# One two-layer diffusion backbone: element-wise work taken off GpSimd, context products moved inside their groups, deeper first loads, the residual loaded by job

## The chip, the core and the metric

The kernel runs on one core of a Trainium2 chip. The metric is the device time of one execution in microseconds (us), from the first to the last instruction and what lies around them; the median of several executions counts. Engines are named as the profile names them: PE is TensorE's matrix products (PEld its weight loads), DVE VectorE, ACT ScalarE, POOL GpSimd, and SP is SyncE, whose queue issues most DMAs.

## What is computed

1024 latent tokens and 256 context tokens of width 1024 pass two layers, all in float32. Layer 0 mixes by four retention heads and four attention heads (two key/value heads) out of one projection; layer 1 by a spatial-gating MLP. Each is followed by a squared-ReLU MLP of width 4096.

```python
def reference(x, c, ctx, c_ctx, mod_w, mod_b, norm1_g, ...):
    for l in range(DEPTH):
        mod_lat = (silu_c @ mod_w[l] + mod_b[l])[:, None, :]      # sh1, sc1, g1, sh2, sc2, g2
        h_lat = modulate(rms_norm(x, norm1_g[l]), sh1, sc1)
        if is_even:
            o_lat, o_ctx = mix_ab(h_lat, h_ctx, ab_w_in[i], ab_w_out[i], ret_decay[i], ...)
        else:
            o_lat = mix_chunk_mlp(h_lat, cm_w_in[i], ...)
        x = x + g1 * o_lat
        x = x + g2 * sq_relu_mlp(modulate(rms_norm(x, norm2_g[l]), sh2, sc2), ff_w1[l], ff_w2[l])

def retention_chunkwise(q, k, v, log_gamma, state0):          # chunks of 128, forward and backward
    scores = jnp.einsum('bnihd,bnjhd->bnhij', qc, kc) * decay
    intra = jnp.einsum('bnhij,bnjhe->bnihe', scores, vc)
    chunk_kv = jnp.einsum('bnjhd,jh,bnjhe->nbhde', kc, k_decay, vc)
    state -> chunk_decay * state + kv_n ;  cross = q @ state_prev * q_decay
```

The first retention state comes from the context tokens; retention and attention queries and keys of the latent tokens are rotated (rotary embedding). Of layer 0 only the latent stream is needed further, so the context runs through the projections alone.

## The kernel before

Every large float32 product is made of three products of rounded pairs (`mm3`, L74: high by high, high by low, low by high). A split into the pair is one ScalarE cast (L80) and one subtraction (L81).

*Start (L106 to L283).* SyncE loads the context, the eight latent tiles `x_t` and sixteen tiles `mw` of the first modulation matrix (two parts of eight; 512 KB each, three buffers, `mod_row`, L235), between them four weight tiles `st` of group 0. TensorE sums the modulation rows (`modrow`), `mod_cols` (L115) turns them into columns; VectorE and ScalarE form squares, and normalise (L266), shift and split the tokens into `hc` (context) and `hl` (latent) (L268 to L280). Of eight row tiles two are split by ScalarE, ScalarE and GpSimd, the others by ScalarE and VectorE.

*Projection groups (L348 to L561).* Six groups: four retention heads (`r_group`) and two key/value groups (`a_group`). `p_group` loads the group's four weight pairs into a ring of twelve tiles, then makes the context's products `pc` (48 instructions) and the latent ones `pl` in four steps `tp` of 48 instructions (two row tiles each), with two accumulators in turn. `lat_evac` empties an accumulator: VectorE makes two rotary products out of it, GpSimd adds them (L485). GpSimd also scales values by their decay (`vc`, L467, of the context; `vk`, L496, of the latent tokens). `tick` advances generators that run beside the group: `heads` of the retention head before, and the transposes `tal`, `tac` of the attention groups.

Between the products of groups 1 to 5 `mod_run` (L156) advances a further generator: 90 steps, ten times eight loads of a 512 KB modulation tile into one of three staging buffers `st`, each with a VectorE multiply-add (`macc`, L139), and a closing step of transposes and sums (`mcol`). The weights use the same three buffers. Two and three steps follow the products of a step `tp` in turn.

*Attention, output product, MLPs.* Scores `s` of attention begin while the last transposes are made. In each layer the MLP's up half writes the hidden tiles to DRAM, seven forms each (`s_d`), out of a ring `ur` of sixteen buffers; the down half (`mlp_down`, L869) reads them back (`sT`, `sB`, L877), multiplies them with seven forms of its weights in jobs (q, p0, p1) and adds each product to the residual `xd` (L882). The residual's eight tiles lie in the space of `ur` and are loaded by GpSimd's queue before the first job, each as soon as its space is free (L944).

The code does not set the order within an engine by itself: a layer underneath records all instructions and fixes each engine's order when the program is built, by their dependences and by estimates of their lengths. Each engine then takes its instructions strictly in that order, and so does SP its DMAs.

```python
            for t in range(2):                       # p_group
                ...
                if gi:
                    mod_run(2 + t)
                tick()
            lat_evac(tp, ps)
```

## Time and profile before

| | |
|---|---|
| median of 3 runs | 2330.74 us (2328.56 to 2338.38) |
| the profiled execution | 2337.72 us, of it 2335.9 us from first to last instruction |
| PE busy | 2243.3 us (96%) |
| DVE busy | 1645.4 us (70%) |
| ACT busy | 1023.4 us (44%) |
| POOL busy | 143.3 us (6%), nearly all of it in the first 470 us |
| granted TensorE clock | 0.982 of full speed |
| moved by DMA | 350.71 MB, 150 GB/s |

The page sums the whole program, so its busy shares mix stages with different limits. The rows further down are from views of single stages: busy time by stretch, what an engine waited for, and single instructions in order of time.

### The profile page before, as it was taken

What the parts mean: (1) busy time and instruction counts of PE and PEld (TensorE: products, weight loads), DVE (VectorE), ACT (ScalarE), POOL (GpSimd) and SP (SyncE); (2) the same over time, 40 slices, a digit from 0 to 9 for tenths busy, and PEclk for the clock granted to TensorE, in tenths of its full rate; (3) what the DMA queues carried; (4) which work ended last, traced back from release to release, by engine and by line L of the source; (5) the groups of instructions that cost most, each with busy time, mean ns of one, the idle gap of its engine ahead of it and who ended that gap; (6) DMA issues with size and microseconds to landing.
All of it is one profiled execution on the core that took longest, in us unless ns stands there. A gap on an engine that the chain in (4) does not pass through costs nothing.

```text
span 2335.9 us, 28819 instructions
## 1 busy us (share of the span) xinstructions
PE 2243.3 (96%) x10412; PEld 1811.7 (78%) x10412; DVE 1645.4 (70%) x2706; ACT 1023.4 (44%) x1809; POOL 143.3 (6%) x133
## 2 busy tenths in 40 slices
PE   6998999889999999999999989999999999899999
PEld 1887888768888788877777867888878888677777
DVE  5666668688857787558877684444678755798785
ACT  3611112267746645554444334323474455544441
POOL 2232321100000000000000010000000000000000
PEclk9998999989999999999999999999999999999999
DMA  8244555430153674456554341115447544754442
GB/s 298 70 144 141 164 189 174 155 129 28 37 194 109 205 236 163 151 197 224 162 148 145 109 158 55 47 45 172 139 144 243 190 152 138 275 162 148 145 139 82
DMA packets 158687, 350.71 MB, mean 150 GB/s; under 512 B 16592, under 2 KB 30416, under 8 KB 158544
## 3 DMA queue, kind: packets, MB, share of 16 engines
q1 hardware_dynamic: 154960, 336.28, 44.7%
q0 software_dynamic: 3584, 12.58, 1.5%
q8 instruction: 82, 1.34, 0.2%
q14 instruction: 61, 0.50, 0.1%
HBM read 262.29 MB, written 86.51 MB: 149 GB/s over the span
## 4 chain that ended last, share of the span: by engine, by line
PE 80%; DVE 8%; DMA 7%; ACT 2%; issue 2%; POOL 1%; SPq 0%; DVEq 0%; ACTq 0%; POOLq 0%
PE ub L77 4%; PE ub L75 4%; PE ub L76 4%; PE dbd L75 4%; PE dbd L76 4%; PE dbd L77 4%; PE po L75 3%; PE po L76 3%; PE po L77 3%; PE ue L75 2%; PE ue L76 2%; PE ue L77 2%; PE pl L77 2%; PE ded L75 2%; PE pl L76 2%; PE pl L75 2%
## 5 line engine op out<-in xcount | busy, mean ns | idle before, releaser
L80 ACT CAST wr<-st 128x512 fp32r<-128x512 f32 (+3 forms) x406 | 278.4, 692 | 490.8 <-PE dbd L76 90.9
L81 DVE TENSOR_TENSOR wr<-st,wr 128x512 fp32r<-128x512 f32 (+3 forms) x402 | 308.4, 774 | 142.7 <-ACT wr L80 124.5
L75 PE MATMUL ub<-T,wr 128*128 128x512 f32 x384 | 153.9, 401 | 8.3 <-DVE ur L822 8.3
L75 PE MATMUL dbd<-sT,wr 128*128 128x512 f32 x384 | 154.0, 402 | 6.2 <-DVE xd L882 6.1
L75 PE MATMUL pl<-wr,h 128*128 128x512 f32 x384 | 155.4, 405 | 0.2 <-ACT zrl L484 0.2
L77 PE MATMUL ub<-T,wr 128*128 128x512 f32 x384 | 153.6, 400 | 0.0
L76 PE MATMUL ub<-T,wr 128*128 128x512 f32 x384 | 153.5, 400 | 0.0
L76 PE MATMUL pl<-wr,h 128*128 128x512 f32 x384 | 153.4, 400 | 0.0
L77 PE MATMUL pl<-wr,h 128*128 128x512 f32 x384 | 153.1, 399 | 0.0
L76 PE MATMUL dbd<-sT,wr 128*128 128x512 f32 x384 | 152.6, 397 | 0.0
L77 PE MATMUL dbd<-sT,wr 128*128 128x512 f32 x384 | 152.1, 397 | 0.0
L882 DVE SCALAR_TENSOR_TENSOR xd<-dbd,mcol,xd 128x512 f32<-128x512 f32 x152 | 112.9, 748 | 44.8 <-PE dbd L77 44.6
L80 ACT CAST sT<-sT 128x512 fp32r<-128x512 f32 x128 | 79.3, 620 | 82.0 <-DMA sT<-s_d 79.3
L139 DVE SCALAR_TENSOR_TENSOR macc<-st,scc,macc 128x1024 f32<-128x1024 f32 x70 | 92.6, 1323 | 24.8 <-DMA st<-in_mod_w 24.4
L81 DVE TENSOR_TENSOR sT<-sT 128x512 fp32r<-128x512 f32 x128 | 87.5, 687 | 19.9 <-ACT sT L80 19.7
L75 PEld LDWEIGHTS dbd<-sT,wr 128*128 128x128 f32 x384 | 72.6, 189 | 30.6 <-DVE xd L882 12.7
L75 PEld LDWEIGHTS ub<-T,wr 128*128 128x128 f32 x384 | 73.1, 190 | 27.3 <-DVE ur L822 9.4
L81 DVE TENSOR_TENSOR sB<-sB 128x512 fp32r<-128x512 f32 x96 | 66.1, 688 | 34.2 <-ACT sB L80 34.0
L791 ACT ACTIVATE ur<-ur 128x512 f32<-128x512 f32 x96 | 60.7, 632 | 64.6 <-DVE ur L837 26.8
L77 PEld LDWEIGHTS ub<-T,wr 128*128 128x128 f32 x384 | 73.2, 191 | 17.5
L76 PEld LDWEIGHTS ub<-T,wr 128*128 128x128 f32 x384 | 73.2, 191 | 17.3
L80 ACT CAST sB<-sB 128x512 fp32r<-128x512 f32 x96 | 59.5, 620 | 61.6 <-DMA sB<-s_d 59.9
(355 smaller groups left out, 5853.2 us busy)
## 6 DMA issues: line engine op xcount, KB each, us to landing
st<-in_w SPq DMA_DIRECT2D x132, 512.0 KB, 4.4
s_d<-ur SPq DMA_DIRECT2D x208, 256.0 KB, 2.3
st<-in_mod_w SPq DMA_DIRECT2D x80, 512.0 KB, 4.4
sT<-s_d SPq DMA_DIRECT2D x128, 256.0 KB, 2.9
sB<-s_d SPq DMA_DIRECT2D x96, 256.0 KB, 3.1
st<-in_wo SPq DMA_DIRECT2D x32, 512.0 KB, 3.6
st<-in_wg SPq DMA_DIRECT2D x24, 512.0 KB, 4.5
mw<-in_mod_w SPq DMA_DIRECT2D x16, 512.0 KB, 5.8
```

Of the source, the lines that this page charges most:

```text
L75: nc.tensor.matmul(ps, lhsT=a_hi, rhs=b_hi, start=first, stop=False, skip_group_check=more)
L76: nc.tensor.matmul(ps, lhsT=a_hi, rhs=b_lo, start=False, stop=False, skip_group_check=more)
L77: nc.tensor.matmul(ps, lhsT=a_lo, rhs=b_hi, start=False, stop=last, skip_group_check=more)
L80: nc.scalar.copy(hi, src)
L81: eng.tensor_tensor(lo, src, hi.bitcast(F32), ALU.subtract)
L139: nc.vector.scalar_tensor_tensor(acc, st, scc[:, k, 0:1], acc, ALU.mult, ALU.add)
L791: nc.scalar.activation(t, t, AF.Relu)
L882: nc.vector.scalar_tensor_tensor(o, ps_, g, o, ALU.mult, ALU.add)
```

## The change

1. Start: six modulation buffers instead of three; the loads are written ahead of the products by six; latent and modulation tiles alternate; the first four weight tiles come after the latent tiles.
2. The split of the first tokens is done by ScalarE and VectorE for all row tiles.
3. The context's products of a group stand before its third step (`at` = 2), in group 0 before its first, in group 5 behind its last.
4. Three modulation steps follow each latent product.
5. The decay scalings go to ScalarE, the rotary sum of the retention groups to VectorE.
6. The residual's tiles are loaded by SyncE in the job that first adds to them, behind that job's hidden tiles.

```diff
@@ start @@
     rows = [mm_tile([2, D], f"modrow{part}") for part in range(2)]
-
-    def mod_row(part, k):
-        st = start.tile([P, WCOL], F32, tag="mw", bufs=3, name=f"mw0_{k}_{part}")
-        nc.sync.dma_start(st, I["mod_w"][0, k * P:(k + 1) * P, part * D:(part + 1) * D])
+    mws = [start.tile([P, WCOL], F32, name=f"mw{i}") for i in range(NMW)]
+    seq = [(part, k) for part in (1, 0) for k in range(KT)]
+
+    def mod_load(i):
+        part, k = seq[i]
+        nc.sync.dma_start(mws[i % NMW], I["mod_w"][0, k * P:(k + 1) * P, part * D:(part + 1) * D])
+
+    def mod_mm(i):
+        part, k = seq[i]
         for j in range(2):
             nc.tensor.matmul(rows[part][:, j * H:(j + 1) * H], lhsT=scc[:, k, :],
-                             rhs=st[:, j * H:(j + 1) * H], start=(k == 0), stop=(k == KT - 1))
+                             rhs=mws[i % NMW][:, j * H:(j + 1) * H], start=(k == 0), stop=(k == KT - 1))
 
     W0 = []
-    for i in range(4):
-        mod_row(1, i)
-        for k in (2 * i, 2 * i + 1):
-            nc.sync.dma_start(x_t[k], I["xT"][k * P:(k + 1) * P, :])
-    pbs = [norm_bc(norm_rstd(start, start_sum(parts[0][0], TC, 0), TC), TC)]
-    for k in range(4, KT):
-        mod_row(1, k)
-        if k == 5:
-            W0.append(p_weight(0, 0))
-    ss_x = start_sum(x_t, T, 1)
-    for k in range(KT):
-        if k == 1:
+    for i in range(2 * KT):
+        if i >= NMW:
+            mod_mm(i - NMW)
+        if i < KT:
+            nc.sync.dma_start(x_t[i], I["xT"][i * P:(i + 1) * P, :])
+        mod_load(i)
+        if i == 4:
+            pbs = [norm_bc(norm_rstd(start, start_sum(parts[0][0], TC, 0), TC), TC)]
+        if i in (8, 10, 12, 14):
+            W0.append(p_weight(0, len(W0)))
+        if i == 8:
+            ss_x = start_sum(x_t, T, 1)
+        if i == KT + NMW - 1:
             mod_cols(1, gs1)
-        if k == 2:
             rs_x = norm_rstd(start, ss_x, T)
-        if k == 3:
             for hf in range(2):
                 pbs.append(norm_bc(rs_x[:, 4 * hf:4 * hf + 4], H))
-        mod_row(0, k)
-        if k in (0, 3, 5):
-            W0.append(p_weight(0, len(W0)))
+    for i in range(2 * KT - NMW, 2 * KT):
+        mod_mm(i)
@@ first tokens' split @@
-                if k % 3 != 2:
-                    nc.scalar.activation(hi, src, AF.Identity, bias=shk)
-                    nc.vector.scalar_tensor_tensor(lo, src, shk, hi.bitcast(F32), ALU.add, ALU.subtract)
-                else:
-                    nc.scalar.activation(src, src, AF.Identity, bias=shk)
-                    split(src, hi, lo, nc.gpsimd)
+                nc.scalar.activation(hi, src, AF.Identity, bias=shk)
+                nc.vector.scalar_tensor_tensor(lo, src, shk, hi.bitcast(F32), ALU.add, ALU.subtract)
@@ p_group @@
-        ps = mm_tile([P, 2, H], f"pc{gi}")
-        for t in range(2):
-            for k in range(KT):
-                hcol = hc[k // 2]
-                mm3(ps[:, t, 0:TC], hcol[:, k % 2, 0, t * P:(t + 1) * P], hcol[:, k % 2, 1, t * P:(t + 1) * P],
-                    wap(k, 0, c0, c0 + TC), wap(k, 1, c0, c0 + TC), k == 0, k == KT - 1)
-        ctx_evac(ps)
-        tick()
+        def ctx_mm():
...
+            tick()
+            return ps
+
+        at = {0: 0, 5: 4}.get(gi, 2)
         for tp in range(4):
+            if tp == at:
+                ctx_evac(ctx_mm())
+                tick()
             ps = mm_tile([P, 2, H], f"pl{gi}_{tp}")
             for t in range(2):
...
                 if gi:
-                    mod_run(2 + t)
+                    mod_run(3)
                 tick()
             lat_evac(tp, ps)
+        if at == 4:
+            ps = ctx_mm()
+            tick()
+            ctx_evac(ps)
@@ r_group: ctx_state, lat_evac, heads @@
-                nc.gpsimd.tensor_scalar(vcs[:, d], z[:, :, P:2 * P], kd[d], None, ALU.mult)
+                nc.scalar.activation(vcs[:, d], z[:, :, P:2 * P], AF.Copy, scale=kd[d])
...
-            nc.gpsimd.tensor_tensor(head_view(z, 0, 2), ta, tb, ALU.add)
+            nc.vector.tensor_tensor(head_view(z, 0, 2), ta, tb, ALU.add)
...
-                    nc.gpsimd.tensor_scalar(vk[:, 2 * tp:2 * tp + 2, :], Z[tp][:, :, TC:TC + P], kd[d], None, ALU.mult)
+                    nc.scalar.activation(vk[:, 2 * tp:2 * tp + 2, :], Z[tp][:, :, TC:TC + P], AF.Copy, scale=kd[d])
@@ mlp_down, layer_mlp @@
-    def mlp_down(l, xt, s_d, done):
+    def mlp_down(l, xt, s_d, x1_d, done):
         S = {}
+        loaded = set()
...
                 if p >= min(p0 for _, p0, _ in parts) and p not in S:
                     load_s(p)
+            for q, _, _ in parts:
+                for m in (q, q + 4):
+                    if m not in loaded:
+                        nc.sync.dma_start(xt[m], x1_d[m])
+                        loaded.add(m)
...
-        for m, x in xt.items():
-            nc.gpsimd.dma_start(x, x1_d[m])
-        left = mlp_down(l, xt, s_d, lambda q, hf: done(q, hf, xt))
+        left = mlp_down(l, xt, s_d, x1_d, lambda q, hf: done(q, hf, xt))
```

Three places in the order of instructions. First SyncE in the start; `mw` are modulation tiles, `x` latent tiles, `st` weight tiles. Before:

```order
L246 DMA x_5_113<-in_xT 128x1024
L237 DMA mw_3_1_162<-in_mod_w 128x1024
L246 DMA x_6_114<-in_xT 128x1024
L246 DMA x_7_115<-in_xT 128x1024
L237 DMA mw_4_1_202<-in_mod_w 128x1024
L237 DMA mw_5_1_206<-in_mod_w 128x1024
L85 DMA st_62<-in_wg 128x2x512
L237 DMA mw_6_1_213<-in_mod_w 128x1024
L237 DMA mw_7_1_217<-in_mod_w 128x1024
L237 DMA mw_0_0_245<-in_mod_w 128x1024
```

With the change, around the first weight tile:

```order
L240 DMA mw_149<-in_mod_w 128x1024
L253 DMA x_6_114<-in_xT 128x1024
L240 DMA mw_144<-in_mod_w 128x1024
L253 DMA x_7_115<-in_xT 128x1024
L240 DMA mw_145<-in_mod_w 128x1024
L240 DMA mw_146<-in_mod_w 128x1024
L86 DMA st_62<-in_wg 128x2x512
L240 DMA mw_147<-in_mod_w 128x1024
L240 DMA mw_148<-in_mod_w 128x1024
L86 DMA st_63<-in_wg 128x2x512
```

Before, two latent tiles went with each modulation tile and the last modulation tiles stood alone; now they alternate one by one. The numbers 144 to 149 are the six buffers in turn.

Next TensorE at the end of group 5; `pl_3` is the last latent product, `tal` the transposes of a step's rotated queries and keys, `s` scores of the first attention head. Before:

```order
L77 MATMUL pl_3_3501<-wr_78,h_1_7_141 128x512
L444 MATMUL tal_2_0_3551<-ident,zal_2_3483 128x128 x3
L444 MATMUL tal_2_1_3556<-ident,zal_2_3483 128x128 x3
L75 MATMUL s_0_0_3618<-wr_70,wr_71 128x256
L76 MATMUL s_0_0_3618<-wr_70,wr_71 128x256
L77 MATMUL s_0_0_3618<-wr_70,wr_72 128x256
L75 MATMUL s_0_0_3619<-wr_68,wr_71 128x512
L76 MATMUL s_0_0_3619<-wr_69,wr_71 128x512
```

With the change, first the end of the latent products, then the end of the context's products:

```order
L78 MATMUL pl_3_3416<-wr_78,h_1_7_141 128x512
L454 MATMUL tal_2_0_3466<-ident,zal_2_3398 128x128 x3
L454 MATMUL tal_2_1_3471<-ident,zal_2_3398 128x128 x3
L76 MATMUL pc_3497<-wr_72,hc_122 128x256
L77 MATMUL pc_3497<-wr_73,hc_122 128x256
L78 MATMUL pc_3497<-wr_72,hc_122 128x256
```

```order
L76 MATMUL s_0_1_3631<-wr_68,wr_71 128x512
L77 MATMUL s_0_1_3631<-wr_69,wr_71 128x512
L78 MATMUL s_0_1_3631<-wr_68,wr_72 128x512
L454 MATMUL tal_3_0_3547<-ident,zal_3_3479 128x128 x3
L454 MATMUL tal_3_1_3552<-ident,zal_3_3479 128x128 x3
L76 MATMUL s_0_0_3608<-wr_70,wr_71 128x256
L77 MATMUL s_0_0_3608<-wr_70,wr_71 128x256
L78 MATMUL s_0_0_3608<-wr_70,wr_72 128x256
L76 MATMUL s_0_1_3630<-wr_70,wr_71 128x256
L77 MATMUL s_0_1_3630<-wr_70,wr_71 128x256
L78 MATMUL s_0_1_3630<-wr_70,wr_72 128x256
L432 MATMUL tac_3652<-ident,zac_3560 128x128 x2
```

The 48 context products `pc` now stand between `tal_2` and the scores; `tal_3` still stands behind twelve score products (the 256-column score products have moved behind it).

Last the residual tiles `xd` of layer 0. Before, they stand alone in GpSimd's queue:

```order
L944 DMA xd_1_8523<-x_d_5596 128x1024
L944 DMA xd_5_8524<-x_d_5596 128x1024
L944 DMA xd_2_8525<-x_d_5596 128x1024
L944 DMA xd_6_8526<-x_d_5596 128x1024
L944 DMA xd_3_8527<-x_d_5596 128x1024
L944 DMA xd_7_8528<-x_d_5596 128x1024
L944 DMA xd_0_8529<-x_d_5596 128x1024
L944 DMA xd_4_8530<-x_d_5596 128x1024
```

With the change they stand in SyncE's queue, between the last hidden tiles that are stored (`s_d_15`), those that are read (`sT`, `sB`) and the weights:

```order
L805 DMA s_d_15_5569<-ur_15_6596 128x512
L888 DMA sT_0_2_8700<-s_d_2_5556 128x512
L888 DMA sB_0_2_8704<-s_d_2_5556 128x512
L888 DMA sB_0_3_8805<-s_d_3_5557 128x512
L903 DMA xd_1_8505<-x_d_5578 128x1024
L903 DMA xd_5_8506<-x_d_5578 128x1024
L903 DMA xd_2_8507<-x_d_5578 128x1024
L903 DMA xd_6_8508<-x_d_5578 128x1024
L903 DMA xd_3_8509<-x_d_5578 128x1024
L903 DMA xd_7_8510<-x_d_5578 128x1024
L888 DMA sT_0_3_8809<-s_d_3_5557 128x512
L888 DMA sB_0_3_8813<-s_d_3_5557 128x512
```

Six tiles follow one another, and the other two stand behind six further hidden pieces.

## Rows read from the trace of the kernel before

**Rows 1.** The page's first part: busy us (share of the span) and instructions.

```profile
PE 2243.3 (96%) x10412; PEld 1811.7 (78%) x10412; DVE 1645.4 (70%) x2706; ACT 1023.4 (44%) x1809; POOL 143.3 (6%) x133
```

**Rows 2.** Busy time by stage; columns end with PE clock, DMA share, GB/s.

```profile
9.10:36.40 27.30, 22.05 (x53) 5.00 (x54) 11.29 (x15) 13.58 (x17) 3.11 (x3) 1.00 0.98 368
36.40:60.00 23.60, 18.99 (x69) 6.45 (x69) 18.84 (x33) 6.09 (x8) 8.62 (x4) 0.90 0.72 228
...
119.60:198.00 78.40, 70.36 (x378) 60.09 (x377) 47.62 (x89) 11.21 (x21) 21.14 (x16) 0.93 0.46 146
198.00:274.00 76.00, 72.86 (x406) 61.84 (x405) 50.59 (x93) 10.87 (x21) 20.44 (x16) 0.98 0.52 156
274.00:346.00 72.00, 68.52 (x380) 58.08 (x378) 50.32 (x91) 10.50 (x20) 20.91 (x16) 0.98 0.55 175
346.00:420.00 74.00, 68.69 (x398) 58.58 (x397) 62.32 (x110) 18.77 (x28) 14.86 (x11) 1.00 0.61 189
420.00:484.00 64.00, 53.33 (x246) 43.63 (x244) 42.69 (x59) 18.53 (x30) 5.98 (x5) 0.90 0.49 158
484.00:498.00 14.00, 10.59 (x46) 8.24 (x45) 12.56 (x27) 12.09 (x23) 0.00 (x0) 0.71 0.65 231
```

**Rows 3.** SyncE's issues in order of time: start us, us, DMA, count.

```profile
36.18 0.43 SPq L85 DMA_DIRECT2D st<-in_wg  x1
41.76 2.04 SPq L237 DMA_DIRECT2D mw<-in_mod_w  x2
```

**Rows 4.** What TensorE waited for to 500 us: us, times, longest.

```profile
PE tal L444 <- ACT av L80: 6.2, 1, 6.2
PE kvc L473 <- POOL vc L467: 5.8, 8, 1.1
PE pc L76 <- DVE wr L81: 5.0, 6, 1.7
PE pc L75 <- ACT wr L80: 3.0, 3, 1.9
...
PE mtp L145 <- DVE macc L139: 2.5, 1, 2.5
```

**Rows 5.** TensorE in order of time, context products of group 0.

```profile
66.97 0.28 PE L77 MATMUL pc<-wr,hc 128*128 128x256 f32 x1
67.09 0.28 PE L75 MATMUL pc<-wr,hc 128*128 128x256 f32 x1
```

**Rows 6.** Groups of instructions and one line: lengths in ns.

```profile
L139 DVE SCALAR_TENSOR_TENSOR macc<-st,scc,macc 128x1024 f32<-128x1024 f32 x70 | 92.6, 1323 | 24.8 <-DMA st<-in_mod_w 24.4
...
L139 DVE SCALAR_TENSOR_TENSOR macc<-st,scc,macc x49: 1265/1284/2194, 116.2 to 343.4; 128x1024 f32<-128x1024 f32 x49
...
L546 DVE TENSOR_TENSOR y<-y,grs 128x512 f32<-128x512 f32 x8 | 5.5, 685 | 1.1 <-POOL grs L541 1.1
...
L484 ACT ACTIVATE zrl<-pl 128x256 f32<-128x256 f32 x16 | 6.3, 391 | 0.0
```

**Rows 7.** DMA issues, 119 to 346 us: count, size, median us to landing.

```profile
st<-in_mod_w SPq DMA_DIRECT2D x54, 512.0 KB, 4.4
```

**Rows 8.** The junctions: stretches, a TensorE wait, a ScalarE cast, the residual's landing.

```profile
1030.00:1110.00 80.00, 73.30 (x296) 58.05 (x295) 63.76 (x103) 40.37 (x75) 3.67 (x7) 0.94 0.69 240
...
1970.00:2045.00 75.00, 68.52 (x280) 54.27 (x279) 54.36 (x90) 38.35 (x70) 3.72 (x7) 0.95 0.69 240
...
1040.00:1050.00 10.00, 8.78 (x38) 6.77 (x36) 4.27 (x7) 5.33 (x11) 1.57 (x3) 1.00 1.02 375
...
PE ub L75 <- DVE ur L822: 4.7, 1, 4.7
...
1049.71 0.62 ACT L80 CAST sT<-sT 128x512 fp32r<-128x512 f32 x1 [4.14 <-DMA sT<-s_d]
...
DMA to landing us min/median/max: 5.0/8.4/11.8
```

More of the change, by code (lines that the diff above doesn't have):

```diff
@@ L29 @@
 NPRO = 8
+NMW = 6
 WCOL = 2 * H
@@ L352, in wap @@
             return W[k // 2][hl_][:, (k % 2) * H + a:(k % 2) * H + b]
-        ps = mm_tile([P, 2, H], f"pc{gi}")
-        for t in range(2):
-            for k in range(KT):
-                hcol = hc[k // 2]
-                mm3(ps[:, t, 0:TC], hcol[:, k % 2, 0, t * P:(t + 1) * P], hcol[:, k % 2, 1, t * P:(t + 1) * P],
-                    wap(k, 0, c0, c0 + TC), wap(k, 1, c0, c0 + TC), k == 0, k == KT - 1)
-        ctx_evac(ps)
-        tick()
+        def ctx_mm():
+            ps = mm_tile([P, 2, H], f"pc{gi}")
+            for t in range(2):
+                for k in range(KT):
+                    hcol = hc[k // 2]
+                    mm3(ps[:, t, 0:TC], hcol[:, k % 2, 0, t * P:(t + 1) * P], hcol[:, k % 2, 1, t * P:(t + 1) * P],
+                        wap(k, 0, c0, c0 + TC), wap(k, 1, c0, c0 + TC), k == 0, k == KT - 1)
+            tick()
+            return ps
+        at = {0: 0, 5: 4}.get(gi, 2)
         for tp in range(4):
+            if tp == at:
+                ctx_evac(ctx_mm())
+                tick()
             ps = mm_tile([P, 2, H], f"pl{gi}_{tp}")
```

## The prediction

> **What bounds the kernel now.** I read the engine shares first. TensorE is busy for 96% of the span [rows 1], so a change can only win the TensorE idle time and the time TensorE ran below its full clock. The table by stage comes next [rows 2]: in each line the stretch less PE's busy time is idle, and the share missing from the granted clock, times the stretch, is what the half clock (1.2 instead of 2.4 GHz) took. Up to 60 us TensorE has little to do and the DMA engines set the pace: 368 GB/s with the queues 98% busy from 9.1 to 36.4 us, but only 228 GB/s at 72% from 36.4 to 60. The five later projection groups and the entry into attention (119.6 to 498 us) lose 8.0, 3.1, 3.5, 5.3, 10.7 and 3.4 us idle, 34.0 in all, and by the clock (0.93, 0.98, 0.98, 1.00, 0.90, 0.71) 5.5, 1.5, 1.4, 0, 6.4 and 4.1 us, 18.9. The list of what TensorE waited for names the causes [rows 4]. The two junctions between the MLP's up and down halves lose 6.7 and 6.5 us idle and 4.8 and 3.8 by the clock [rows 8]. All that the change can reach is thus about 9 + 53 + 22 us; the attention, output products and MLP bodies are untouched.
>
> My sums stand against the profiled execution, 2337.7 us, which is 7.0 us above the median of 2330.7; I take the 7.0 off at the end. From no change a measurement here can tell about 0.5%, 11.7 us.
>
> **The start.** SyncE may have only three modulation tiles in flight. Behind the issue at 36.18 it sends nothing until 41.76 us, because each load waits until TensorE has used the tile three places earlier [rows 3]. With six tiles the loads run on. Bytes are the same: the 23.6 us of the third stretch carry 228 x 23.6 = 5.4 MB, which at the second stretch's 368 GB/s take 14.6 us, so 9.0 us is the most [rows 2]. Below, nothing: latent and modulation tiles now alternate one by one, and after eight of each the same bytes are in. I take 7, since the transposes and shifts behind the last tile stay as long as they are. The eight split pieces that move from GpSimd to VectorE there cost nothing while VectorE is busy 18.8 of 23.6 us or less; if VectorE were full they would cost about eight times 0.7 [rows 2, 6].
>
> **GpSimd off the retention.** Eight times TensorE waited for the scaled context values, 5.8 us [rows 4]. ScalarE now makes them, 0.39 us for such a shape [rows 6], and is busy 11 us of a 76 us group [rows 2]; the 40 pieces add 16 us to it over four groups. Hidden; gain 5.8, at worst 0 if ScalarE waits in its queue for VectorE.
>
> VectorE takes over 16 rotary sums. None of that shape with two inputs from SBUF stands in the group's rotary step; the nearest row is the 128x512 product at 0.685 us [rows 6], so 2.7 us a group. The modulation steps move as well: three follow each latent product instead of two and three in turn, 24 a group instead of 20. Groups 1 to 3 get four more each, at most 4 x 1.28 = 5.1 us [rows 6], and the 90 steps end in group 4 instead of 5. VectorE in groups 1 to 3 goes from 47.6, 50.6 and 50.3 us to about 55 to 58 of 72 to 78. Group 4 today shows what a fuller VectorE costs: 62.3 of 74 us and 5.3 us of TensorE idle [rows 2]. If groups 1 to 3 went there from nothing, 16 us; if their slack holds, 0. I take 6, nearer the slack. Queued behind a modulation step that waits for its load are the rotary products that empty the accumulators, and TensorE waits for those.
>
> GpSimd running beside VectorE has a price too, and it is small: of the modulation products the median takes 1284 ns, the mean 1323, the slowest 2194 [rows 6]; 70 x 0.04 = 2.7 us back. The Trainium skill (SBUF — State Buffer, Who interferes with whom) says that a VectorE instruction with two SBUF inputs contends with a GpSimd instruction that reads SBUF, and that the loser is blocked for the whole instruction; by that up to GpSimd's 62 busy us of groups 1 to 3 would come back to VectorE. The trace does not agree with so much; the rule's full size is the rival "port" below.
>
> **Context products moved.** At a group's start the weights are still being split, and the context products, which ran first, use up a weight pair with six instructions of 0.12 us [rows 5]; the latent ones, with 512 columns for 256, take about twice that. So each further pair is asked for some 0.7 us later, and the waits of 5.0 and 3.0 us for weights [rows 4] should about halve: 4, between 0 (they move to the first latent products) and 8. In the last group the 48 context products, 48 x 0.12 = 5.8 us, move behind the last latent product. There TensorE stood 6.2 us before the last transposes (the row's releaser is named after a neighbour on the same semaphore; what they need is the last rotary sum), and 2.5 us for a modulation sum that is now gone from this group [rows 4]. 5.8 + 2.5 and some 4 of the 10.5 us that the clock took in the last two lines [rows 2], rounded: 12. At least 0, at most the 24.6 lost there. What is late next is the softmax of the first score tiles, which keeps its wait. For the clock in groups 1 to 3 I add 2 of 8.4, since its drops follow idle time and some of that stays.
>
> **The residual.** Today GpSimd's queue asks for the residual tiles when their space comes free, three of 512 KB at 1040 us, into DMA queues that are 102% busy at 375 GB/s; there the wait of 4.7 us falls, for an add that VectorE holds behind a split whose cast on ScalarE stood 4.1 us for its load [rows 8]. The change sends them from SyncE, behind the first hidden tiles: 1.6 MB, 4.2 us at that rate, leave the busiest stretch. They come back before the first down products end, and the loads' median landing of 8.4 us [rows 8] then lies near the first accumulation. On SyncE they stand in front of the next weight loads and delay those by eight issues of 0.43 us [rows 3], 3.4 us, while GpSimd's queue is left with the stores of the finished rows alone. I take +5 for both layers. Ends: all 21.8 us lost at both junctions, or the landing in full on the path, 8.4 twice, minus 16.8.
>
> **Sum.** 7 + 6 + 4 + 12 + 2 + 5 - 6 = 30. 2337.7 - 30 = 2307.7 for such an execution, and 2301 beside the median. By itself, with the middle of each range, 2289 to 2313.
>
> **Rivals.**
> - *VectorE full.* Groups 1 to 3 cost the whole 16 to 18 us instead of 6: gain 18, 2313. For: VectorE already stands 24.4 us for modulation loads [rows 6], with everything behind it. Against: two accumulator tiles and 14 us of slack a group.
> - *Residual late.* The first add of a job waits for its tile: -9 instead of +5, gain 16, 2315. For: 8.4 us landing. Against: in the new SyncE order the tiles stand ahead of the last hidden pieces, so these are later still. Both of these together: gain 4, 2327.
> - *Slower: the three staging buffers.* A modulation tile holds its buffer for landing plus product, 4.4 + 1.28 us [rows 6, 7], so three buffers pass 25 tiles (24 steps hold 21 loads, and four weight pairs) in 47 us, which fits in a 72 us group. Were the landing over 9.3 us, the 25 tiles would need 88 us, the weights of the next group would come late, and 3 x 16 us would eat all gains and more. At 9.8 us: 92 us, 60 lost against 36 gained, 24 slower, 2355. For: 4.4 is a median with 150 to 190 GB/s, and the demand rises by a sixth. Against: the queues stay near half busy [rows 2].
> - *Port.* VectorE is freed of all blocking: no cost of 6, and the idle and clock losses up to 420 us (19.9 + 8.4) vanish. 7 + 28 + 12 + 5 = 52, 2279. For: the slow products. Against: their median. The rule of the Trainium skill named above (SBUF — State Buffer, Who interferes with whom) would have it so.
>
> **How the numbers follow.** Forecast 0.57, port 0.06, VectorE full 0.14, residual late 0.10, both 0.06, slower 0.07. Faster than 2319 holds the first two, nearly all of the third and most of the fourth: 0.84; within 0.5% the rest of these and the case of both, 0.09; slower 0.07. The range runs from 2278 (the port case inside) to 2330 (both inside); the slower case and the fringes of the forecast stay out.
>
> **What would show it.** Right: the context products of the first group about 7 us earlier, the one at 66.97 [rows 5] before 61; no wait for context values; TensorE idle under 7 us in the last group and the entry; the modulation products over before the last group starts; the wait of 4.7 us at the first junction gone or under 2. Wrong: groups 1 to 3 longer than 78, 76 and 72 us with TensorE waiting for VectorE; the first accumulations of the down half waiting for a residual load; the start no shorter, which would say that bytes and not depth set it.

## The result, and the profile after

The changed kernel takes 2296.99 us (2295.74 to 2297.41, four runs) against 2331.03 us of the kernel before (2328.56 to 2338.38, four runs): ratio 0.9856, 95% interval 0.9839 to 0.9872. Forecast were 2301 us, range 2278 to 2330. The profiled execution took 2295.74 us, its span 2293.9.

First part of the page and one line of its DMA issues, changed kernel:

```profile
PE 2224.5 (97%) x10412; PEld 1799.8 (78%) x10412; DVE 1646.8 (72%) x2730; ACT 1034.7 (45%) x1839; POOL 53.3 (2%) x53
...
st<-in_mod_w SPq DMA_DIRECT2D x80, 512.0 KB, 4.4
```

GpSimd's busy time falls from 143.3 to 53.3 us [rows 1]; of the 143.3, 113.4 lay in the first 470 us and 29.9 behind them, which is more than "nearly all" leaves. VectorE's total, which took over the rotary sums, stays where it was. The modulation tiles still land in 4.4 us [rows 7], so the slow case with three staging buffers did not come.

Busy time by stage, changed kernel (columns as in [rows 2]: stretch, length, busy us of PE, PEld, DVE, ACT, POOL, then clock, DMA share, GB/s): the start in two stretches, group 2, the last group up to the first softmax wait, the entry into attention:

```profile
9.10:36.40 27.30, 23.38 (x70) 7.03 (x70) 15.15 (x24) 13.62 (x17) 4.71 (x4) 1.00 1.03 407
36.40:54.00 17.60, 15.55 (x50) 5.75 (x50) 14.17 (x25) 5.63 (x7) 7.03 (x3) 0.90 0.78 270
173.10:246.30 73.20, 68.74 (x390) 59.13 (x390) 56.39 (x107) 16.65 (x33) 3.02 (x3) 0.98 0.60 195
387.80:452.00 64.20, 58.80 (x304) 49.36 (x303) 37.23 (x53) 19.39 (x30) 7.32 (x6) 1.00 0.34 109
452.00:466.00 14.00, 8.99 (x44) 7.37 (x44) 13.44 (x28) 13.89 (x28) 0.00 (x0) 0.76 0.80 281
```

The start ends 5.8 us earlier than in the trace of before (54.0 for 59.8 us): the queues are full at 407 GB/s instead of 368 in the first of its stretches, and the second is shorter [rows 2]. In the last group and the entry TensorE is idle for 5.4 + 5.0 us. What it still waits for, from the list of its waits up to 500 us:

```profile
PE s L76 <- ACT pr L617: 5.0, 1, 5.0
PE py L560 <- DVE y L556: 3.8, 4, 1.7
PE mtp L146 <- DVE hms L412: 2.9, 1, 2.9
PE tal L454 <- DVE zal L445: 2.2, 1, 2.2
...
PE pl L77 <- DVE wr L82: 1.1, 1, 1.1
PE pl L76 <- ACT wr L81: 0.8, 1, 0.8
```

Context values (5.8 us) are gone from it, and so is the wait of 6.2 us before the last transposes; weights cost some 3 us for 8 [rows 4]. New at the top is the first softmax (5.0), and waits for the heads' results (`y`, `hms`) of VectorE have taken some of the room.

Two further marks that the prediction named, the 33rd context product of group 0 and the first and last start of the modulation products (one line's instructions: shortest, median, longest ns):

```profile
61.54 0.28 PE L78 MATMUL pc<-wr,hc 128*128 128x256 f32 x1
```

```profile
L140 DVE SCALAR_TENSOR_TENSOR macc<-st,scc,macc x70: 1257/1284/1291, 109.8 to 368.6; 128x1024 f32<-128x1024 f32 x70
```

The first stood at 66.97 us [rows 5], so it comes 5.4 us earlier, and the sign "before 61" is missed by half a microsecond. The second ends before the last group's first latent product (389.8 us), and its longest fell from 2194 to 1291 ns [rows 6].

### The profile page after: what moved, and what is told of

Its sections match the earlier page's. It is cut to its first block, busy times and chain, and to the rows that moved or that the text cites. A ratio compares the mean times of both kernels' runs of the same rounds, so it can differ in the third digit from the quotient of the medians.

```text
span 2293.9 us, 28755 instructions
## 1 busy us (share of the span) xinstructions
PE 2224.5 (97%) x10412; PEld 1799.8 (78%) x10412; DVE 1646.8 (72%) x2730; ACT 1034.7 (45%) x1839; POOL 53.3 (2%) x53
## 5 line engine op out<-in xcount | busy, mean ns | idle before, releaser
L81 ACT CAST wr<-st 128x512 fp32r<-128x512 f32 (+2 forms) x406 | 278.8, 692 | 456.6 <-PE dbd L77 85.7
L82 DVE TENSOR_TENSOR wr<-st,wr 128x512 fp32r<-128x512 f32 (+2 forms) x402 | 307.7, 772 | 134.1 <-ACT wr L81 92.9
L76 PE MATMUL dbd<-sT,wr 128*128 128x512 f32 x384 | 153.9, 401 | 10.8 <-DVE xd L893 10.5
L76 PE MATMUL pl<-wr,h 128*128 128x512 f32 x384 | 153.1, 400 | 1.5 <-ACT wr L81 0.8
L76 PE MATMUL ub<-T,wr 128*128 128x512 f32 x384 | 152.2, 396 | 0.6 <-DVE ur L822 0.6
L77 PE MATMUL pl<-wr,h 128*128 128x512 f32 x384 | 151.3, 394 | 1.1 <-DVE wr L82 1.1
L77 PE MATMUL ub<-T,wr 128*128 128x512 f32 x384 | 151.9, 395 | 0.0
L78 PE MATMUL ub<-T,wr 128*128 128x512 f32 x384 | 151.9, 395 | 0.0
L78 PE MATMUL pl<-wr,h 128*128 128x512 f32 x384 | 150.6, 393 | 0.0
L140 DVE SCALAR_TENSOR_TENSOR macc<-st,scc,macc 128x1024 f32<-128x1024 f32 x70 | 89.8, 1283 | 20.2 <-DMA st<-in_mod_w 19.6
L76 PEld LDWEIGHTS dbd<-sT,wr 128*128 128x128 f32 x384 | 72.4, 188 | 35.3 <-DVE xd L893 17.9
L76 PEld LDWEIGHTS ub<-T,wr 128*128 128x128 f32 x384 | 72.2, 188 | 19.2 <-ACT wr L81 1.9
L78 PEld LDWEIGHTS dbd<-sT,wr 128*128 128x128 f32 x384 | 72.3, 188 | 17.5
L78 PEld LDWEIGHTS ub<-T,wr 128*128 128x128 f32 x384 | 72.2, 188 | 17.4
L76 PEld LDWEIGHTS pl<-wr,h 128*128 128x128 f32 x384 | 72.8, 189 | 16.6 <-ACT wr L81 1.2
```

The source lines that it names most:

```text
L76: nc.tensor.matmul(ps, lhsT=a_hi, rhs=b_hi, start=first, stop=False, skip_group_check=more)
L77: nc.tensor.matmul(ps, lhsT=a_hi, rhs=b_lo, start=False, stop=False, skip_group_check=more)
L78: nc.tensor.matmul(ps, lhsT=a_lo, rhs=b_hi, start=False, stop=last, skip_group_check=more)
L81: nc.scalar.copy(hi, src)
L82: eng.tensor_tensor(lo, src, hi.bitcast(F32), ALU.subtract)
L140: nc.vector.scalar_tensor_tensor(acc, st, scc[:, k, 0:1], acc, ALU.mult, ALU.add)
```

## The experiments

The medians below stand beside the changed kernel's 2297.0; the interval of each ratio is about 0.17% wide to each side, some 4 us, so that single steps under 4 us rest on the traces, not on the times. Those of the kernel before on the same chips were 2329.7 to 2330.6 us. Each variant has one trace, and traces differ by themselves: the two of the kernel before by 7.8 us of span.

### The kernel before, once more

> The kernel before, unchanged, for a second trace. Theory (the profiled execution of before lay 7.0 us above its median because TensorE's clock was lowered for longer in the entry into attention and at the junctions): the span is some 2322 to 2330 us, the start (first context product at 59.8 us) and the six groups as long as before within 2 us, and the difference lies in the stretches at 1.2 GHz. Rival (the difference lies in waits of the groups): the waits for weights, for the last transposes and for the modulation sum differ by several us.

One execution: 2329.85 us, span 2328.1. The trace shown first was 7.8 us longer: 3.3 of that lie between the fifth group's end and the first up product (368.7 for 365.4 us, with 10.2 for 6.8 us lost by the clock), 4.0 in the two down halves, while the start and the first five groups agree within 2 us. Over the whole span the half clock took 41.2 us there and 32.4 here. The theory holds for this pair of traces, and the second trace is the fairer one to measure the change against. From it to the changed kernel, stage by stage in us: start 6.7, groups 0 to 4 6.4, last group with attention and output product 14.3, up halves 4.4 and 5.4, down halves -2.6 and -2.3, the spatial-gating part 1.8; together 34.1, the difference of the spans.

### The start

```diff
-    mws = [start.tile([P, WCOL], F32, name=f"mw{i}") for i in range(NMW)]
+        st = start.tile([P, WCOL], F32, tag="mw", bufs=3, name=f"mw0_{k}_{part}")
```

and the loop of before with it.

> The changed kernel with the old start: three buffers for the first modulation matrix, one such load to two latent tiles, weight tiles between. The first tokens are still split by ScalarE and VectorE alone. Theory (depth set the start): the first context product, at 54.0 us now, comes at 59 to 60 us, 2302 to 2304. Rival (what comes earlier is given back as waits for the weights of group 0, whose loads now come last): 2297 to 2299. Rival (the split by VectorE was what gained): the first context product at 54 to 56.

2299.7 us (ratio 0.9881, 0.9863 to 0.9899), less than the theory's loss; but the first context product comes at 61.7 us, later than it said. SyncE's issues and the second stretch of this kernel:

```profile
36.66 0.43 SPq L86 DMA_DIRECT2D st<-in_wg  x1
40.55 2.04 SPq L238 DMA_DIRECT2D mw<-in_mod_w  x2
42.65 0.43 SPq L86 DMA_DIRECT2D st<-in_wg  x1
46.06 2.04 SPq L238 DMA_DIRECT2D mw<-in_mod_w  x2
```

```profile
36.40:61.70 25.30, 19.24 (x77) 6.69 (x75) 18.68 (x33) 6.36 (x9) 8.70 (x4) 0.93 0.73 232
```

SyncE stands again between the modulation loads, as in [rows 3], at 232 GB/s. Depth and order of the loads, undone together, are worth 7.7 us at the first product, and the split by VectorE is not what gained. No run has the one without the other. The time shows 2.7 of these 7.7; by the trace group 0 takes back 1.2 (52.6 for 53.8 us), the rest is within what two executions differ by.

### The residual

```diff
-                        nc.sync.dma_start(xt[m], x1_d[m])
+        for m, x in xt.items():
+            nc.gpsimd.dma_start(x, x1_d[m])
```

> The changed kernel with the residual loaded as before: all eight tiles by GpSimd's queue, each as soon as its space is free. The changed kernel takes 2297 us. Theory (the junctions' gain, 5.7 us to the first down product of layer 0 and 4.7 to that of layer 1, comes from taking the residual's early tiles out of the busiest stretch of the queues): both waits of TensorE in the last up products come back (4.7 and 3.6 us before), the late waits for the first addition (3.9 and 3.7 us now) go: 2303 to 2308. Rival (the gain there came from the clock or from another order, and the residual's move has cost the late waits): they go and nothing comes back, 2288 to 2292.

2301.9 us (ratio 0.9881, 0.9863 to 0.9899), just under the theory's range. From the first up product to the first down product it takes 289.9 and 284.1 us for 282.9 and 281.3 of the changed kernel; the down halves are 2.6 and 1.3 us shorter. Both waits in the up half are back (4.0 and 2.6 us), but of the two late ones only that of layer 0 is gone: in layer 1 TensorE still waits 3.9 us for an addition. A cast on ScalarE, a wait of TensorE and ten microseconds of the busiest stretch, this kernel:

```profile
1020.17 0.62 ACT L81 CAST sT<-sT 128x512 fp32r<-128x512 f32 x1 [4.41 <-DMA sT<-s_d]
```

```profile
1023.32 0.80 PE L76 MATMUL ub<-T,wr 128*128 128x512 f32 x1 [4.00 <-DVE ur L832]
```

```profile
1010.00:1020.00 10.00, 9.32 (x40) 7.16 (x39) 4.38 (x8) 5.23 (x10) 1.58 (x3) 1.00 1.02 359
```

This is the picture of [rows 8]: the residual in full queues, a hidden tile 4.4 us late, TensorE behind it. The theory's mechanism holds for the up half. On SyncE the same place is free (the list of TensorE's waits has none there), and in layer 0 the wait stands in the down half instead. SyncE, ScalarE, VectorE and TensorE of the changed kernel there:

```profile
1029.11 3.99 SPq L903 DMA_DIRECT2D xd<-x_d  x6
```

```profile
1034.31 0.62 ACT L81 CAST sB<-sB 128x512 fp32r<-128x512 f32 x1 [0.75 <-DMA sB<-s_d]
```

```profile
1034.96 0.69 DVE L82 TENSOR_TENSOR sB<-sB 128x512 fp32r<-128x512 f32 x1 [0.68 <-ACT sB L81]
1035.62 0.75 DVE L893 SCALAR_TENSOR_TENSOR xd<-dbd,mcol,xd 128x512 f32<-128x512 f32 x1
```

```profile
1036.43 0.50 PE L76 MATMUL dbd<-sT,wr 128*128 128x512 f32 x1 [3.94 <-DVE xd L893]
```

Is it the residual tile that the first addition (1035.62) waits for, or the split in front of it? In this trace the two end together: the tile, asked for at 1029.11, lands at 1035.60. In layer 1 of the same kernel the tile is the later one, by the 1.23 us that VectorE stands idle before the addition, of 3.6 us of TensorE's wait:

```profile
1978.33 0.75 DVE L893 SCALAR_TENSOR_TENSOR xd<-dbd,mcol,xd 128x512 f32<-128x512 f32 x1 [1.23 <-DMA xd<-x_d]
```

The next kernel asks for the tiles of the first two additions early (and SyncE leaves these two out):

```diff
+        for m in (1, 2):
+            nc.gpsimd.dma_start(xt[m], x1_d[m])
```

> The changed kernel with two of the residual's eight tiles, those that the first two additions need (x1 and x2), asked for by GpSimd's queue as soon as their space is free; the six others stay on SyncE in their jobs. Theory (the first addition now waits for its residual tile, 3.9 and 3.7 us of TensorE, and 1 MB early is little enough): the late waits go, 2289 to 2292. Rival (any residual load in the stretch where the hidden tiles come back delays them): a wait in the last up products comes back and takes the gain, 2295 to 2301.

2299.1 us (ratio 0.9863, 0.9844 to 0.9883). The last of the two is asked for at 1009.05 us, and such loads land in 4.7 to 6.6 us. GpSimd, VectorE and TensorE of this kernel:

```profile
1009.05 0.53 POOL L960 DMA_DIRECT2D xd<-x_d  x1 [19.82 <-DMA s_d<-ur]
```

```profile
1034.84 1.38 DVE L82 TENSOR_TENSOR sB<-sB 128x512 fp32r<-128x512 f32 x2 [0.68 <-ACT sB L81]
1036.13 0.74 DVE L893 SCALAR_TENSOR_TENSOR xd<-dbd,mcol,xd 128x512 f32<-128x512 f32 x1
```

```profile
1036.93 0.80 PE L76 MATMUL dbd<-sT,wr 128*128 128x512 f32 x1 [3.20 <-DVE xd L893]
```

The tile had lain there for 20 us, and the addition started as late as before. Both expectations were wrong: no wait above 0.6 us came back in the up half, and the late one stayed, 3.2 us in each layer for 3.9 and 3.6. The addition stands in VectorE's order behind splits of hidden tiles that come late out of full queues (their share is 0.96 and 0.98 from 1030 to 1035 us in the two kernels). The residual's landing is a second bound beside it: equal in layer 0 of the changed kernel, 1.2 us later in layer 1.

### The last group's context products

```diff
-        at = {0: 0, 5: 4}.get(gi, 2)
+        at = {0: 0, 5: 0}.get(gi, 2)
```

> The changed kernel with the context products of the last group ahead of its first latent product, as before; in groups 1 to 4 they stay before the third step. The last group and the entry into attention gained 17.6 us against the profiled execution of before. Theory (the 48 products behind the last latent product cover the wait for the last rotary sum): a wait of some 6 us before the last transposes comes back, with clock loss behind it, 2303 to 2309. Rival (it is the modulation, gone from the last group, that gave it): at most 2 us, 2296 to 2299.

2296.7 us (ratio 0.9856, 0.9837 to 0.9875): no difference, as the rival had it for the time. Two rows of TensorE's waits from 390 to 470 us:

```profile
PE tal L454 <- ACT av L81: 6.1, 1, 6.1
PE s L76 <- ACT pr L617: 2.7, 1, 2.7
```

The wait before the last transposes came back in full, as the theory had it. But the softmax wait behind it fell from 5.0 to 2.7, and the trace of this kernel is only 3.1 us longer between the fifth group's end and the first up product.

### GpSimd's part

```diff
-                nc.scalar.activation(vcs[:, d], z[:, :, P:2 * P], AF.Copy, scale=kd[d])
+                nc.gpsimd.tensor_scalar(vcs[:, d], z[:, :, P:2 * P], kd[d], None, ALU.mult)
```

and likewise `vk` and the rotary sum of `zrl`.

> The changed kernel with the decay scalings of the context's and the latent values and the rotary sums of the retention groups on GpSimd again. Theory (what was gained is the wait for the scaled context values, 5.8 us, and slow VectorE instructions beside GpSimd, some 40 ns for each modulation product; VectorE's relief of 16 sums a rotary step is small): 2299 to 2305, eight waits of 0.2 to 1.1 us for the context values, mean of the modulation products 1320 ns again. Rival port (VectorE is blocked whenever GpSimd works): groups 1 to 3 lose all that GpSimd is busy there, 2315 or more. Rival VectorE full (the sums on VectorE cost more than the waits): 2291 to 2296.

2299.7 us (ratio 0.9863, 0.9841 to 0.9884). One of the two forecast causes is there (modulation products of 1346 ns in the mean for 1283), the other hardly: one wait of 1.0 us for context values and one of 2.5 for latent ones. That GpSimd has more time for them, with the context products inside the group, would explain it; no run tests this alone.

### Modulation and context

```diff
-                    mod_run(3)
+                    mod_run(2 + t)
```

> The changed kernel with two and three modulation steps after the latent products in turn, as before, so that the last ten of the 90 steps fall into the last group again. Moving the context products of the last group back cost nothing, so its 17.6 us have another source. Theory (it is the modulation gone from the last group: a wait for a modulation sum, VectorE's queue ahead of the rotary sums, and the clock behind it): 2302 to 2308, less 2 to 4 us that groups 1 to 3 give back. Rival (VectorE fuller costs as much in groups 1 to 3 as the emptied last group gains): 2295 to 2299. Rival (fuller costs more): 2291 to 2294.

2300.2 us (ratio 0.9875, 0.9856 to 0.9894): between the theory and the first rival. Groups 1 to 3 gave nothing back; they are 1.2 us longer in the trace (207.2 for 206.0).

```diff
-        at = {0: 0, 5: 4}.get(gi, 2)
+        at = 0
```

with one advance of the generators (`tick`) behind the products, as before, where the change makes two.

> The changed kernel with the context products ahead of the first latent product in all six groups, as before; the last group alone made no difference. Theory (in groups 1 to 4 the products that ran first asked for weight pairs faster than VectorE and ScalarE split them): the waits for weights at the group starts come back, 8.0 us in all before, 2300 to 2305. Rival (they were moved, not removed, or the six-instruction use is not what sets them): 2295 to 2299.

2293.3 us (ratio 0.9842, 0.9826 to 0.9859): not slower than the changed kernel, rather faster, though the intervals overlap; below both expectations. Single parts undone thus cost 2.7, 4.9, 2.7, 3.2 and -3.7 us, 9.8 of 34. So several were undone at once.

### Several parts at once

> The changed kernel with three parts undone at once: the retention's element-wise work on GpSimd again, two and three modulation steps in turn, context products first in all groups. What stays of the change is the start, the split of the first tokens and the residual. Undone one by one the three cost 2.7, 3.2 and -3.7 us, while the six groups and attention together are 20.7 us shorter than in the second trace of the kernel before. Theory (each part covers for the others, and all of the gain is in these three): 2297 + 20.7, 2314 to 2321. Rival (the parts add up): 2297 to 2302, and the groups' gain has another source, the shorter start or the split of the first tokens.

2321.6 us (twelve runs, 2316.1 to 2331.3; ratio 0.9961, 0.9948 to 0.9974). It lies 0.6 us above the theory's range, and far from the rival: these three parts hold 24.6 of the 34 us.

> The changed kernel with two of the three parts undone: modulation steps in turn and context products first; GpSimd stays off the retention's element-wise work. Theory (GpSimd's part carries the groups' gain: no wait for context values, no slow VectorE instructions, and with these the waits for weights, sums and transposes fall): 2294 to 2301. Rival (the three are alike, any two suffice): 2297 to 2303. Rival (the moves of modulation and context carry it): 2308 or more.

2303.9 us (ratio 0.9882, 0.9866 to 0.9898): GpSimd's part alone gives 17.8 us, a little less than the theory and the first rival said. Between the two traces it is 12.7 (spans of 2315.7 and 2303.0 us), and groups 1 to 3 alone hold more than that: 4.6 us of waits for context values, 3.5 of waits for VectorE (its modulation sum and a head's result), 5.1 by the clock.

> The changed kernel with GpSimd's element-wise work back and the context products first; three modulation steps after each latent product stay. Theory (GpSimd's part carries the gain): the eight waits for context values come back, 5.8 us, beside slow modulation products and what hangs on them, 2306 to 2314. Rival (any one of the three suffices): 2296 to 2302. With the runs so far this also tells what moving the context products does while GpSimd works (against 2299.7 with GpSimd's part alone undone).

2299.3 us (ratio 0.9863, 0.9845 to 0.9881). Here the theory is wrong and the rival right: the waits for context values are back, and yet the modulation's three steps alone gain 22.3 us. Together, with the stage lengths that the times of the last latent products and of the first up product give in each trace:

| kernel | GpSimd off | three steps | context moved | us | groups 1 to 3 | group 4 to the first up product | waits for weights |
|---|---|---|---|---|---|---|---|
| before, second trace | | | | 2329.9 | 215.6 | 435.7 | 7.7 |
| u_pmc | no | no | no | 2321.6 | 213.8 | 435.0 | 8.9 |
| u_mc | yes | no | no | 2303.9 | 200.1 | 439.3 | 10.5 |
| u_pc | no | yes | no | 2299.3 | 206.7 | 427.7 | 2.0 |
| u_mod | yes | no | yes | 2300.2 | 207.2 | 426.7 | 3.2 |
| u_pool | no | yes | yes | 2299.7 | 209.8 | 426.2 | 0.9 |
| u_ctx | yes | yes | no | 2293.3 | 201.1 | 427.5 | 3.7 |
| changed kernel | yes | yes | yes | 2297.0 | 206.0 | 425.1 | 2.6 |
| n_best (below) | yes | yes | last group | 2290.1 | 206.3 | 420.3 | 0.9 |

The last column is what TensorE waited for weights in its context and latent products from 85 to 480 us. Where the context products are not moved, the generators also advance once behind them; in the three rows of moved ones and in n_best they advance twice. How far traces differ by themselves: five with the same code in groups 1 to 3 (the changed kernel, u_start, u_res, n_mix, u_ctx5) took 204.4 to 206.0 us there; the two of the kernel before agree within 0.1 us there, but not from group 4 to the first up product (440.5 and 435.7).

From group 4 to the first up product either the three steps or the moved context products give 7 to 13 us, and both together hardly more: they take away the same loss. The waits for weights are about half of it: in groups 4 and 5 they fall from 4.4 us (u_pmc) to 1.3 (u_pc), and from 6.6 (u_mc) to 0.9 (u_ctx) and 0.6 (u_mod). In groups 1 to 3 GpSimd's part gives 13.7 alone and 5.6 beside the three steps, and the moved context products with their second advance cost 3 to 7. TensorE's waits in u_pmc, u_pc and u_ctx from 85 to 480 us, in this order, show what each took away:

```profile
PE kvc L482 <- POOL vc L476: 6.8, 7, 2.1
...
PE pc L77 <- DVE wr L82: 4.5, 5, 1.8
PE pc L76 <- ACT wr L81: 4.4, 3, 3.5
```

```profile
PE kvc L482 <- POOL vc L476: 6.6, 8, 1.6
...
PE pc L77 <- DVE wr L82: 1.0, 2, 0.9
PE pc L76 <- ACT wr L81: 1.0, 2, 0.6
```

```profile
PE pc L77 <- DVE wr L82: 2.8, 4, 0.9
...
PE pc L76 <- ACT wr L81: 0.9, 1, 0.9
...
PE kvc L482 <- ACT vc L476: 0.2, 1, 0.2
```

GpSimd's part takes the waits for context values, and beside the three steps they match its whole worth: 6.6 to 0.2 us by the waits, 6.0 by the times. The waits for weights (8.9 us) go with the modulation's steps, without any move of the context products (2.0). Of the 8.9, 3.8 stood in the last group, and none of the 2.0. Why, SyncE's loads of the last group's weights show, in u_pmc and in u_pc:

```profile
382.37 6.42 SPq L136 DMA_DIRECT2D st<-in_mod_w  x4
...
392.14 3.39 SPq L86 DMA_DIRECT2D st<-in_wg  x2
...
397.21 0.37 SPq L86 DMA_DIRECT2D st<-in_wg  x1
...
400.51 0.38 SPq L86 DMA_DIRECT2D st<-in_wg  x1
```

```profile
371.00 2.45 SPq L86 DMA_DIRECT2D st<-in_wg  x2
...
374.38 5.86 SPq L86 DMA_DIRECT2D st<-in_wg  x2
```

Group 4's last latent product ends at 394.0 and 387.6 us. Where modulation tiles still pass through the same three staging buffers, the four loads go out up to 6.5 us after that; where the modulation is over, 7.7 to 16.6 us ahead of it. In group 2, where modulation runs in both kernels, the last of the four goes out 6.6 and 2.7 us after group 1's end, and the waits there are 3.5 and 0.8 us.

### A version that beats both

```diff
-        at = {0: 0, 5: 4}.get(gi, 2)
+        at = {5: 4}.get(gi, 0)
```

> The changed kernel with the context products first in groups 0 to 4 and behind the last latent product in the last group. Theory (undone in all groups the move gained 3.7 us, 2293.3; in the last group it covers the wait for the last transposes, 3 us by the traces of both): 2289 to 2292. Rival (the last group gives nothing, as its own run said): 2292 to 2295.

2290.1 us (five runs, 2288.7 to 2293.7; ratio 0.9825, 0.9809 to 0.9841): the lowest median, 6.9 us below the changed kernel. Its lead of 3.2 us over u_ctx is not shown: the intervals overlap, and of the two traces that of u_ctx is the shorter (2289.0 for 2291.9 us). Against u_ctx the last group gives what the theory said (350.4 for 354.7 us from group 4's end to the first up product). Against the changed kernel it gains from group 4 on (420.3 for 425.1), 4.1 of these 4.8 us in group 4 itself (69.9 for 74.0); what gained there no run separates. It does not gain in groups 1 to 3, although its context products stand first there like those of u_ctx (201.1). What u_ctx has beyond it in these groups is one advance of the generators behind the context products instead of two; so the second advance, not the place of the products, is what the comparison points to as the cost of 5 us, three times what traces of the same code differ by there. No kernel with the moved products and one advance was run, nor n_best with one.

## Why the prediction was right, point by point

Time and sign were right, and so was the mechanism of three terms: the start, GpSimd and the residual. That the sum came out as well as it did is partly luck. For groups 0 to 4 it holds +6, -6, +4 and +2, together 6, and 6.4 came; but three of these four were off, and the errors cancelled. And the parts were added up as if independent, which three of them are not.

- **The start, +7.** 5.8 us at the first context product against the first trace, 6.7 against the second, 7.7 by undoing it. The loads were the cause; that it was their depth and not their order is argued from SyncE's stops between them. The second stretch did not reach the 368 GB/s of the estimate (270), but the first moved more (407).
- **GpSimd off the retention, +6.** The wait went for good, 6.6 to 0.2 us, and ScalarE's pieces were hidden, though each takes 0.51 us and not 0.39. Right in size only beside the three steps; alone GpSimd's part gives 12.7 us by the traces and 17.8 by the times, 6.4 of them by these waits.
- **VectorE fuller, -6.** Too dear. With GpSimd off, three steps instead of two and three make groups 1 to 3 1.0 us longer (200.1 to 201.1) and group 4 1.7; with the context products moved, 1.2 shorter and 4.4 longer (u_mod against the changed kernel). The case "VectorE full" fell with it. VectorE is 56.4 us busy in the 73.2 of group 2, as forecast, and the slack carried it; what I did not see is that the step pays.
- **Context products moved, +4 at the group starts.** The wrong term. The waits fell, but the step that failed is to count their fall as this move's own gain, from the one cause that "the context products, which ran first, use up a weight pair with six instructions". The other cause is when the loads go out, and the staging buffers and SyncE's queue, shared with the modulation, set that: the three steps alone took the waits from 8.9 to 2.0 us (u_pc), and from 10.5 to 3.7 with GpSimd off (u_ctx). The move alone took them from 10.5 to 3.2 (u_mod), beside the three steps only from 3.7 to 2.6. Whether its share comes from larger products in front, as the prediction says, or from the second advance, no run tells: n_best, with the products first and two advances, has 0.9. What the sum left out costs more than the move gives: groups 1 to 3 are some 5 us longer with the second advance.
- **Last group and entry, +12.** 14.3 us, or 10.6 with group 4, which is 3.7 us longer. The wait of 6.2 us is covered as forecast, and the softmax came next. But the sum took the move (5.8), the modulation (2.5) and the clock (4) as independent, and left out the weights of this group (2.6 us of waits in the second trace, none now). They are not independent: either the moved products or the three steps give most of it, which is why undoing the first changed nothing. And TensorE's idle time there stayed at 10.4 us, above the 7 forecast.
- **Clock in groups 1 to 3, +2.** 3.4 us against the second trace (5.1 to 1.7); the five traces with the changed kernel's code there have 0 to 1.7.
- **The residual, +5.** 4.9 us by undoing it, 4.9 by the stages (4.4 - 2.6 + 5.4 - 2.3). Its loss in the down half, 3.9 and 3.6 us of TensorE, is the sign "first accumulations waiting for a residual load" in part: the tile is the last bound in layer 1, for 1.2 us, and ties in layer 0. n_mix showed that without it splits of late hidden tiles still hold the addition for 3.2 us. So the rival "residual late" was right that something would be late, mostly wrong about what, and too dear.
- **The port.** Its full size did not come: beside the three steps GpSimd costs 6.0 us (u_pc against u_ctx), and the waits for context values account for that. The 3.5 us of waits for VectorE that went with GpSimd's part alone may be its doing; no run tells. What the case had wrong is who loses: where the two engines met it was mostly GpSimd that waited (last section).

## What to carry to other kernels

Where several parts of a change take away the same loss, undoing one shows little: here single parts cost -4 to 5 us, three together 25. Undo them in combinations before calling one useless. Here a background stream that shares staging buffers and a queue with the next stage's weights delayed that stage, whatever its own engine time; ending it a stage earlier helped. And a load asked for earlier helps only if the instruction that needs it does not stand behind another late one on its engine.

## What the hardware showed beyond that

With GpSimd at work the modulation product has the same median but a longest of 2285 ns. This one, on VectorE, and GpSimd beside it, in u_pc:

```profile
204.78 2.29 DVE L140 SCALAR_TENSOR_TENSOR macc<-st,scc,macc 128x1024 f32<-128x1024 f32 x1
```

```profile
204.69 1.29 POOL L494 TENSOR_TENSOR zrl<-ropea,ropeb 128x512 f32<-128x512 f32 x1 [3.12 <-DVE ropeb L399]
205.96 1.90 POOL L505 TENSOR_SCALAR vk<-zrl,kdec 128x256 f32<-128x256 f32 x1
```

Another product, and GpSimd beside it:

```profile
147.77 1.27 DVE L140 SCALAR_TENSOR_TENSOR macc<-st,scc,macc 128x1024 f32<-128x1024 f32 x1
```

```profile
147.93 2.26 POOL L494 TENSOR_TENSOR zrl<-ropea,ropeb 128x512 f32<-128x512 f32 x1 [12.93 <-DVE ropeb L399]
```

In the first pair the sum began first, kept its 1.29 us, and the product took 1.0 us longer. In the second the product began first, kept its 1.27 us, and the sum took 2.26 for 1.29. Of the seventy products of this kernel six span the passage from a GpSimd sum (TENSOR_TENSOR) to a scaling (TENSOR_SCALAR), and these took 1.35 to 2.29 us; 21 others that ran beside one or the other took 1.25 to 1.42, and the 43 beside neither 1.27 to 1.29. GpSimd fared worse: all 18 of its sums and scalings that began inside a product, more than 0.1 us before its end, took 0.5 to 1.0 us longer than the shortest of their kind (1.28 and 0.92 us). A scaling already under way held a product up by 0.14 us at most, a sum by up to 1.0; in u_pool three products of 2.20 us ran beside sums alone.

The Trainium skill (SBUF — State Buffer, Who interferes with whom) says that a VectorE instruction with two SBUF inputs contends with a GpSimd instruction that reads SBUF. The trace agrees, except for products that began inside a scaling. VectorE loses little by it, 94.3 us of products for the 89.6 of u_ctx, where GpSimd does none of this work, because it is mostly GpSimd's instruction that began later and waited: its 56 instructions took 76.2 us, some 19 more than at their shortest.
